# The head of an encoder-layer kernel: inputs and small vectors asked for by GpSimd, own landing tiles for the first projections' weights, and the next weights asked for inside the head

## The chip, the cores and the metric

The kernel runs on one core of one Trainium2 chip. The time is the device time of one execution in microseconds (us), and smaller is better. The kernel before took 2841.35 us (median of three runs, 2839.85 to 2841.55).

## The reference, cut to what matters

One layer of a hybrid encoder is computed for 512 prompt rows and 64 sample rows, each 2048 wide, in float32:

```python
def trunk(x, c, states, params, block):
    ...
        mod = jax.nn.silu(c) @ w_ada[l] + b_ada[l]
        sh1, sc1, g1, sh2, sc2, g2 = jnp.split(mod[:, None, :], N_MOD, axis=-1)
        h = rmsnorm(x, norm1[l]) * (1 + sc1) + sh1
        mix, s_a, s_b, s_c = token_mixers(
            h, gla_s[l], gdn_s[l], conv_s[l], w_in[l], gla_wg[l], gla_bg[l], gla_norm[l],
            gdn_conv_w[l], gdn_a_log[l], gdn_dt_bias[l], gdn_norm[l], w_out[l], block)
        x = x + g1 * mix
        h = rmsnorm(x, norm2[l]) * (1 + sc2) + sh2
        f, s_f = conv_ffn(h, ffn_s[l], w_up[l], ffn_conv_w[l], ffn_conv_b[l], w_down[l])
        x = x + g2 * f
    ...
def token_mixers(h, ...):
    proj = h @ w_in
    (a_q, a_k, a_v, a_r, a_lr, b_q, b_k, b_v, b_g, b_beta, b_alpha) = jnp.split(
        proj, IN_OFFSETS, axis=-1)
    ...
    g = -jnp.exp(gdn_a_log.astype(f32))[:, None, None] * jax.nn.softplus(
        to_heads(b_alpha, GDN_HEADS) + gdn_dt_bias.astype(f32)[:, None, None])
```

Before the first projection `h @ w_in` can start, two of the six parts of `mod` are needed, the shift `sh1` and the scale `sc1`. Each is a product of the two vectors `c` (prompt and sample) with a 2048 x 2048 piece of `w_ada`, so 32 MB of weights are read for two vectors. The other four parts are needed later and are computed beside the projections.

## The kernel before, in words

Activations lie with features on the 128 partitions, so `h` is 16 tiles of 128 x 576 (two halves of 288). Every float32 product is made of three matmuls on pairs of a rounded high part and its rest: `hh` times `wh`, `hl` times `wh`, `hh` times `wl` (function `mm6`, lines 560 and 562, six matmuls of 288 columns for one tile of 128 x 128 weights). A weight tile is loaded to a landing tile, ScalarE makes the high part and VectorE the rest (function `split`, lines 647, 649 and 650).

The first stage is the function `head`. Its work runs in four groups of four feature tiles. For each group g the function `modulation(g)` reads 16 pieces of `w_ada`, 512 KB each (line 751), eight for the scale and eight for the shift; for each piece TensorE makes four matmul instructions with the vectors `c` (line 755). After eight pieces VectorE copies the sum out (line 757), TensorE turns it (line 760), and VectorE adds the bias (line 806). Then `split_mod` forms `hh` and `hl` of the four tiles (lines 582 to 585), and TensorE multiplies them with the narrow columns (`mm_narrow`, line 886) and with the q and k columns of the first head (lines 560 and 562). The x rows are loaded in five blocks (line 697), turned to feature-major by TensorE (line 705), and normed on the way.

The pieces of `w_ada` land in a ring of buffers that is named by the letters of `RING`: `a` is the head's own `hraw` (five buffers), `h` and `l` are the places of split weights `wh` and `wl` (three each), and `r` is the common landing tile `raw` (three). The narrow, q and k weights of a group also land in `raw`.

Before the change all loads and stores of the head are asked for by one queue, SyncE's (SP), in program order as a scheduler lays it out. That scheduler orders each engine's instructions by what it thinks is ready, and `split` raises its own priority by `AHEAD`. An engine then works strictly in that order. A load waits in the queue until its buffer is free, and at most eight transfers of a queue's kind are under way, since each takes one of eight semaphores and waits for the one before it on the same semaphore.

After the head, `gdn_heads` runs the projections head by head, each a `gemm` over 16 tiles. Between the first two, `narrow` makes the decay of all heads: it adds `gdn_dt_bias` to a narrow product, takes a softplus, and sums along the rows by a matmul with a triangle (line 933). `x` is also written to memory for the residual (`xs`, line 799), and `gdn_dt_bias` and `gdn_a_log` are loaded at lines 902 and 903.

## Time and profile before

| what | value |
|---|---|
| median of three runs | 2841.35 us |
| profiled execution | 2845.19 us |
| its span, first to last instruction | 2843.4 us |
| mean granted TensorE clock | 0.988 |
| TensorE busy | 2786.9 us (98%) |
| VectorE busy | 2248.6 us (79%) |
| ScalarE busy | 1293.8 us (46%) |
| GpSimd busy | 316.3 us (11%) |
| moved by DMA | 399.78 MB, mean 141 GB/s |

The page gives the busy time of each engine over the span, then the same in 40 slices. The first two slices (142 us) differ from the rest: there the DMA engines move 322 and 343 GB/s, more than twice what they move later. The later slices have TensorE busy at nine tenths or more. Line numbers are those of the kernel before unless it is said otherwise.

### The profile page before, as it was taken

The page shows a single profiled execution, that of the slowest core. Times are in us where ns is not written, and L with a number is a line of the kernel's source. Part 1 is how long each engine was busy: PE and PEld are TensorE (multiplying, and loading weights), DVE is VectorE, ACT ScalarE, POOL GpSimd, SP SyncE. Part 2 cuts the span into 40 slices and gives each one's busy share as a digit, 9 for nine tenths or more (in the row PEclk, how much of TensorE's full clock was granted, in tenths as well). Part 3 has the DMA queues.
Part 4 walks back from the last instruction along what each step waited for, and adds up shares of the span by engine and source line. Part 5 has one row for each costly group of instructions (what it writes and reads, how often), then busy time and mean ns, then how long its engine had stood idle before and what let it go on. Part 6 is the DMA issues. An engine that isn't in the chain of part 4 may idle for free.

```text
span 2843.4 us, 51759 instructions
## 1 busy us (share of the span) xinstructions
PE 2786.9 (98%) x20560; PEld 2690.0 (95%) x20560; DVE 2248.6 (79%) x3728; ACT 1293.8 (46%) x2285; POOL 316.3 (11%) x586
## 2 busy tenths in 40 slices
PE   7999999999999999999999999999999999999998
PEld 3699999999999999999999999999999999999997
DVE  2488888787777787468888888888878889999995
ACT  4275555444433333255444444444444464434453
POOL 0024433332010001001000000000000000000000
PEclk8999999999999999999999999999999999999999
DMA  9964555555455449333333333333333343443461
GB/s 322 343 189 144 168 155 167 144 154 162 124 149 175 141 143 262 107 111 97 107 105 111 102 104 107 108 104 102 102 104 108 105 151 116 123 124 119 128 171 68
DMA packets 522440, 399.78 MB, mean 141 GB/s; under 512 B 50794, under 2 KB 453957, under 8 KB 522197
## 3 DMA queue, kind: packets, MB, share of 16 engines
q1 hardware_dynamic: 516772, 385.79, 45.7%
q0 software_dynamic: 5424, 10.68, 1.2%
q8 instruction: 162, 2.65, 0.4%
q14 instruction: 82, 0.66, 0.1%
HBM read 356.24 MB, written 40.13 MB: 139 GB/s over the span
## 4 chain that ended last, share of the span: by engine, by line
PE 76%; DVE 4%; DMA 2%; issue 1%; ACT 1%; POOL 0%; SPq 0%; ACTq 0%; DVEq 0%; POOLq 0%
PE g L560 16%; PE g L1381 9%; PE g L1382 8%; PE g L1383 8%; PE g L562 8%; PE bank L1382 3%; PE bank L1381 3%; PE bank L1383 3%; PE g L1616 3%; PE g L1614 3%; PE g L1615 3%; DVE wl L1566 1%; PE bank L1616 1%; PE bank L1614 1%; PE bank L1615 1%
## 5 line engine op out<-in xcount | busy, mean ns | idle before, releaser
L1381 PE MATMUL g<-slot,wh 128*128 128x290 f32 x1760 | 533.4, 303 | 3.1 <-ACT p L1393 3.1
L1382 PE MATMUL g<-slot,wh 128*128 128x290 f32 x1760 | 525.9, 299 | 0.0
L1383 PE MATMUL g<-slot,wl 128*128 128x290 f32 x1760 | 520.4, 296 | 0.0
L560 PE MATMUL g<-hh,wh 128*128 128x288 f32 x1984 | 450.5, 307 | 1.1 <-ACT hh L1168 0.8
L562 PE MATMUL g<-hh,wl 128*128 128x288 f32 x1984 | 432.8, 299 | 0.0
L560 PE MATMUL g<-hl,wh 128*128 128x288 f32 x1984 | 432.1, 298 | 0.0
L1328 ACT ACTIVATE wh<-raw 128x1024 fp32r<-128x1024 f32 x176 | 186.7, 1061 | 391.8 <-PE g L1382 369.5
L1381 PEld LDWEIGHTS g<-slot,wh 128*128 128x128 f32 x1760 | 331.5, 188 | 17.5 <-ACT p L1393 12.0
L1383 PEld LDWEIGHTS g<-slot,wl 128*128 128x128 f32 x1760 | 336.6, 191 | 0.0
L1382 PEld LDWEIGHTS g<-slot,wh 128*128 128x128 f32 x1760 | 335.1, 190 | 0.1
L560 PEld LDWEIGHTS g<-hh,wh 128*128 128x128 f32 x1984 | 320.5, 191 | 3.8 <-ACT hh L1168 1.0
L560 PEld LDWEIGHTS g<-hl,wh 128*128 128x128 f32 x1984 | 322.7, 190 | 0.2 <-issue 0.2
L562 PEld LDWEIGHTS g<-hh,wl 128*128 128x128 f32 x1984 | 321.3, 190 | 0.5 <-DVE wl L650 0.3
L649 ACT ACTIVATE wh<-raw 128x1024 fp32r<-128x1024 f32 x147 | 156.0, 1061 | 313.3 <-PE g L560 284.2
L829 DVE SCALAR_TENSOR_TENSOR acc<-xr,ct,acc 128x512 f32<-128x512 f32 x322 | 230.3, 747 | 1.5 <-DMA xr<-in_w_ada_dram 1.5
L1329 DVE TENSOR_TENSOR wl<-raw,wh 128x1024 fp32r<-128x1024 f32 x176 | 214.5, 1219 | 19.3 <-ACT wh L1328 19.2
L1614 PE MATMUL g<-slot,wh 128*128 128x288 f32 x760 | 224.4, 295 | 0.9 <-DVE slot L1631 0.9
L1616 PE MATMUL g<-slot,wl 128*128 128x288 f32 x760 | 224.0, 295 | 0.3 <-DVE wl L1566 0.3
L1615 PE MATMUL g<-slot,wh 128*128 128x288 f32 x760 | 224.2, 295 | 0.0
L650 DVE TENSOR_TENSOR wl<-raw,wh 128x1024 fp32r<-128x1024 f32 x147 | 179.4, 1221 | 41.8 <-ACT wh L649 41.2
L1382 PE MATMUL bank<-slot,wh 128*128 128x290 f32 x704 | 210.1, 298 | 0.0
L1381 PE MATMUL bank<-slot,wh 128*128 128x290 f32 x704 | 209.4, 297 | 0.0
(418 smaller groups left out, 5926.2 us busy)
## 6 DMA issues: line engine op xcount, KB each, us to landing
raw<-in_w_up_dram SPq DMA_DIRECT2D x176, 512.0 KB
raw<-in_w_in_dram SPq DMA_DIRECT2D x108, 512.0 KB
xr<-in_w_ada_dram SPq DMA_DIRECT2D x86, 512.0 KB
raw<-in_w_down_dram SPq DMA_DIRECT2D x76, 512.0 KB
ax<-in_w_ada_dram SPq DMA_DIRECT2D x42, 512.0 KB
raw<-in_w_out_dram SPq DMA_DIRECT2D x32, 512.0 KB
hraw<-in_w_ada_dram SPq DMA_DIRECT2D x23, 512.0 KB
actd<-v SPq DMA_DIRECT2D x44, 256.0 KB
```

The lines of the kernel that those rows point to most:

```text
L560: T.matmul(ps[:, h if bank is None else bank, :n], wh, x[:, h, :n], start=f, stop=False)
L562: T.matmul(ps[:, h if bank is None else bank, :n], wl, ah[:, h, :n], start=False, stop=stop)
L650: nc.vector.tensor_tensor(lo[:, :n_], raw[:, :n_], hi[:, :n_].bitcast(F32), op=ALU.subtract)
L829: V.scalar_tensor_tensor(acc[s], w[:, k], col, acc[s], op0=ALU.mult, op1=ALU.add)
L1328: self.nc.scalar.activation(hi, src, AF.Copy)
L1329: self.nc.vector.tensor_tensor(lo, src, hi.bitcast(F32), op=ALU.subtract)
L1381: T.matmul(ps, wh[:, j], hi, start=(c < 3 and j == 0), stop=False, skip_group_check=True)
L1382: T.matmul(ps, wh[:, j], lo, start=False, stop=False, skip_group_check=True)
L1383: T.matmul(ps, wl[:, j], hi, start=False, stop=(j == NPAIR - 1), skip_group_check=True)
L1614: T.matmul(ps, wh[:, j, f], hi, start=(c < 3 and j == 0), stop=False, skip_group_check=True)
L1615: T.matmul(ps, wh[:, j, f], lo, start=False, stop=False, skip_group_check=True)
L1616: T.matmul(ps, wl[:, j, f], hi, start=False, stop=(j == n - 1), skip_group_check=True)
```

## The change

- The five blocks of x are asked for by GpSimd's queue, all in the first five steps of the first modulation, instead of by SyncE's in steps 1, 3, 5, 7 and 9. The vectors are asked for by GpSimd too, but for the first group (the two vectors `c`), which ScalarE's queue asks for.
- `RING` is now a finite list of 64 letters: 48 that repeat a pattern of thirteen (four `a`, three each of `h`, `l` and `r`), then 16 without `r`. `hraw` has four buffers instead of five.
- The q and k weights of a group land in a tile kind of their own, `fr`, with four buffers. They are asked for, with the narrow ones, before the pieces of `w_ada` of the next group.
- The split weights of the second head's q projection, both halves, and the first half of its k projection are asked for in group 3 of the head. Before, only the two q halves were, behind the head.
- All writes of `xs` come behind the last piece of `w_ada`. Before, one came in the first group, and the others behind the head.
- `gdn_dt_bias` and `gdn_a_log` are loaded by GpSimd in the head to a tile that lasts (`row8`).
- The copy `rw` of a modulation sum goes to the tile `junk`, which the norms of x also use as a place for values that nobody reads.

```diff
-RING = "ahlarahlahralr"
+RING = "ahlrahlrahlra" * 4
+RING = RING[:48] + "hlahlahlahlahlaa"
...
-                nc.sync.dma_start(rt[at:at + n], ap)
+                (nc.scalar if g == 0 else nc.gpsimd).dma_start(rt[at:at + n], ap)
...
+        self.row8 = self.cp.tile([P, 16], F32, name="row8")
...
-        turns = iter(RING * 99)
+        turns = iter(RING)
...
-            return pool.tile([P, 1024], F32, tag="hraw", bufs=5, name=self.name("hraw"))
+            return pool.tile([P, 1024], F32, tag="hraw", bufs=4, name=self.name("hraw"))
...
+        fraw = lambda: pool.tile([P, 512], F32, tag="fr", bufs=4, name=self.name("fr"))
+        free = [fraw()]
...
-                nc.sync.dma_start(xt[b][q][:n], i["x_prompt"][0, b * P:(b + 1) * P, f] if b < 4 else i["x_sample"][0, :, f])
+                nc.gpsimd.dma_start(xt[b][q][:n], i["x_prompt"][0, b * P:(b + 1) * P, f] if b < 4 else i["x_sample"][0, :, f])
...
-                rw = pool.tile([P, 512], F32, tag="rw", bufs=1, name=self.name("rw"))
+                rw = junk
                 V.tensor_copy(rw, ps)
...
-                for _ in vectors:
-                    pass
             self.scale_mod(s1, 1, "norm1", 4 * g)
...
-            for f, at in ((x_load, 0), (x_turn, X_LAG), (x_norm, X_LAG + 1)):
-                plan[X_AT[b] + at].append(lambda f=f, b=b: f(b))
+            for f, at in ((x_load, b), (x_turn, X_AT[b] + X_LAG), (x_norm, X_AT[b] + X_LAG + 1)):
+                plan[at].append(lambda f=f, b=b: f(b))
         step = iter(plan)
         modulation(0, lambda: [f() for f in next(step)])
+        for c, name in ((0, "gdn_dt_bias"), (8, "gdn_a_log")):
+            nc.gpsimd.dma_start(self.row8[:, c:c + 8], i[name].partition_broadcast(P).rearrange("p a b -> p (a b)"))
+        for _ in vectors:
+            pass
         rx = x_rows()
...
+        self.pre = []
         for g in range(4):
+            ks = range(4 * g, 4 * g + 4)
+            nar = self.narrow_w(pool, 4 * g)
+            ws = [self.split(pool, self.w_in(off)(4 * g, 4 * g + 4), "f", 512, 3, free.pop() if free else fraw())
+                  for off in (OFF_BQ, OFF_BK)]
             if g < 3:
                 modulation(g + 1)
-            ks = range(4 * g, 4 * g + 4)
-            nar = self.narrow_w(pool, 4 * g)
-            qw, kw = [self.split(pool, self.w_in(off)(4 * g, 4 * g + 4), "f", 512, 3) for off in (OFF_BQ, OFF_BK)]
+            else:
+                self.load_consts(None, NARROW)
+                for off, k0 in ((OFF_BQ + P, 0), (OFF_BQ + P, 8), (OFF_BK + P, 0)):
+                    self.pre.append(self.wtile(self.w_in(off)(k0, k0 + 8)))
             for k in ks:
...
-                if k == 0:
-                    nc.sync.dma_start(self.xs[KD - 1], xT[:, KD - 1])
...
-        self.load_consts(None, NARROW)
-        rest = [*range(2, KD - 1), 0, 1]
-        self.pre = []
-        for k0 in (None, 0, 8):
-            if k0 is not None:
-                self.pre.append(self.wtile(self.w_in(OFF_BQ + P)(k0, k0 + 8)))
-                last[0] = self.load_of
-            with self.tc.issue_after(last[0]):
-                for k in rest[:5]:
-                    nc.sync.dma_start(self.xs[k], xT[:, k])
-            rest = rest[5:]
+        with self.tc.issue_after(last[0]):
+            for k in (*range(KD - 3, KD), *range(KD - 3)):
+                nc.sync.dma_start(self.xs[k], xT[:, k])
...
-        row = g("row8", 16)
-        nc.sync.dma_start(row[:, 0:8], i["gdn_dt_bias"].partition_broadcast(P).rearrange("p a b -> p (a b)"))
-        nc.sync.dma_start(row[:, 8:16], i["gdn_a_log"].partition_broadcast(P).rearrange("p a b -> p (a b)"))
+        row = self.row8
```

The scheduler makes new orders of this. Three places matter below. In the rows a name's last number counts allocations, so the same weights bear other numbers in the two kernels.

The first place is SyncE's queue at the start of the program (`hs` are tiles of x; `hraw`, `wh`, `wl` and `raw` hold pieces of `w_ada`). Before:

```order
L751 DMA hraw_214<-in_w_ada_dram 128x2x512
L697 DMA hs_222<-in_x_prompt_dram 128x512
L697 DMA hs_223<-in_x_prompt_dram 128x512
L697 DMA hs_224<-in_x_prompt_dram 128x512
L697 DMA hs_225<-in_x_prompt_dram 128x512
L751 DMA wh_230<-in_w_ada_dram 128x2x512
L751 DMA wl_236<-in_w_ada_dram 128x2x512
```

And now, from the eighth piece of `w_ada` to behind the first weights of the projections:

```order
L755 DMA raw_352<-in_w_ada_dram 128x2x512
L755 DMA hraw_390<-in_w_ada_dram 128x2x512
L755 DMA wh_400<-in_w_ada_dram 128x2x512
L755 DMA wl_430<-in_w_ada_dram 128x2x512
L755 DMA raw_440<-in_w_ada_dram 128x2x512
L648 DMA fr_216<-in_w_in_dram 128x4x128
L648 DMA fr_557<-in_w_in_dram 128x4x128
L755 DMA hraw_468<-in_w_ada_dram 128x2x512
```

Twelve pieces of `w_ada` now stand in a row where x stood between them, and the q and k weights of group 0 come 13th and 14th; x stands in GpSimd's queue behind three vectors and a memset.

The second place is TensorE's order at the third modulation, of group 2 (`bank` is a modulation sum, `fh` and `nar` are weights of the projections). Before, the pieces stand in a row, and the products of group 1 come behind most of them:

```order
L760 MATMUL bank_781<-consts_95,rw_779 128x2 x4
L755 MATMUL bank_787<-wl_788,cst 32x512 x2
L755 MATMUL bank_787<-raw_790,cst 32x512 x2
L755 MATMUL bank_787<-hraw_796,cst 32x512 x2
L755 MATMUL bank_787<-wh_798,cst 32x512 x2
L755 MATMUL bank_787<-wl_804,cst 32x512 x2
L755 MATMUL bank_787<-hraw_806,cst 32x512 x2
L755 MATMUL bank_787<-raw_812,cst 32x512 x2
L560 MATMUL g_542<-hh_848,fh_837 128x288 x2
```

Now the products of group 1 start right behind the turn of its own shift, and the first eight pieces of the next modulation stand singly among them:

```order
L764 MATMUL bank_637<-consts_95,hs_218 128x2 x4
L561 MATMUL g_544<-hh_844,fh_752 128x288 x2
L561 MATMUL ps_k_221<-hh_844,fh_758 128x288 x2
L888 MATMUL g_543<-hh_844,nar_745 66x288 x2
L888 MATMUL g_543<-hl_845,nar_745 66x288 x2
L561 MATMUL g_544<-hl_845,fh_752 128x288
L759 MATMUL bank_763<-wl_764,cst 32x512 x2
L561 MATMUL g_544<-hl_845,fh_752 128x288
L563 MATMUL g_544<-hh_844,fl_753 128x288 x2
L561 MATMUL ps_k_221<-hl_845,fh_758 128x288 x2
L759 MATMUL bank_763<-raw_766,cst 32x512 x2
```

The eight pieces of the shift then stand in a row behind the last product of the group. The order in groups 0 and 2 has the same form.

The third place is TensorE's order behind the head, in the second head's q projection, where the matmul with the triangle (`ln` with `xr`) stands. Before:

```order
L560 MATMUL g_1432<-hh_1125,wh_1288 128x288 x2
L560 MATMUL g_1432<-hl_1126,wh_1288 128x288 x2
L933 MATMUL bank_1384<-ln,xr_1269 128x32
L934 MATMUL bank_1384<-ln,xr_1269 128x4
L562 MATMUL g_1432<-hh_1125,wl_1289 128x288 x2
```

Now:

```order
L563 MATMUL g_1430<-hh_1119,wl_1173 128x288 x2
L561 MATMUL g_1430<-hh_1183,wh_1172 128x288 x2
L933 MATMUL bank_1382<-ln,xr_1163 128x32
L934 MATMUL bank_1382<-ln,xr_1163 128x4
L561 MATMUL g_1430<-hl_1184,wh_1172 128x288 x2
```

It moved back by two rows, to behind the twelfth tile's products and one pair. From the 1675th matmul instruction on (of 19595), TensorE's order is the same in both kernels.

More of the change, by code (lines that the diff above doesn't have):

```diff
@@ L784, in head @@
                 self.h.append((hh, hl))
-                if k == 0:
-                    nc.sync.dma_start(self.xs[KD - 1], xT[:, KD - 1])
                 self.mm_narrow(k, nar[:, k % 4])
-                for ps, w in ((self.ps_q0, qw), (ps_k0, kw)):
+                for ps, w in zip((self.ps_q0, ps_k0), ws):
                     self.mm6(ps, w[0][:, k % 4], w[1][:, k % 4], self.h[k], k == 0, k == KD - 1)
-        self.load_consts(None, NARROW)
-        rest = [*range(2, KD - 1), 0, 1]
-        self.pre = []
-        for k0 in (None, 0, 8):
-            if k0 is not None:
-                self.pre.append(self.wtile(self.w_in(OFF_BQ + P)(k0, k0 + 8)))
-                last[0] = self.load_of
-            with self.tc.issue_after(last[0]):
-                for k in rest[:5]:
-                    nc.sync.dma_start(self.xs[k], xT[:, k])
-            rest = rest[5:]
+        with self.tc.issue_after(last[0]):
+            for k in (*range(KD - 3, KD), *range(KD - 3)):
+                nc.sync.dma_start(self.xs[k], xT[:, k])
         raw = self.xr()
```

## The prediction

> **What bounds the kernel now.** I read the slices of the page first, then stages of the start, then TensorE's (PE) rows in order of time, then the queue's waits. The slices show where PE is not full:
>
> ```profile
> PE   7999999999999999999999999999999999999998
> DMA  9964555555455449333333333333333343443461
> ```
>
> Only the first slices have PE below nine tenths and the DMA engines near full. So I cut the start into stages. A boundary is where the turn of a shift ends (line 760, groups 0 to 3), then the head's last product, then the first transposes of the second head. Columns: PE, weight load, VectorE (DVE), ScalarE (ACT), GpSimd (POOL), granted clock, DMA share, GB/s.
>
> ```profile
> 0.00:10.00 10.00, 3.12 (x9) 1.12 (x10) 0.74 (x6) 2.33 (x5) 1.25 (x7) 1.00 0.60 185
> 10.00:25.00 15.00, 12.80 (x71) 6.11 (x69) 1.38 (x8) 13.11 (x34) 1.11 (x2) 1.00 1.05 395
> 25.00:35.00 10.00, 8.20 (x41) 3.81 (x37) 2.90 (x13) 5.56 (x15) 1.10 (x2) 0.83 0.78 228
> 35.00:48.65 13.65, 12.02 (x62) 4.79 (x64) 3.04 (x8) 3.84 (x12) 0.54 (x1) 0.75 1.03 387
> 48.65:76.97 28.32, 23.88 (x105) 8.97 (x104) 10.33 (x23) 5.31 (x11) 0.00 (x0) 0.76 0.98 351
> 76.97:99.14 22.17, 20.00 (x141) 11.96 (x141) 10.57 (x24) 5.33 (x11) 0.32 (x1) 1.00 1.07 381
> 99.14:125.15 26.01, 24.23 (x162) 14.82 (x163) 10.57 (x24) 5.33 (x11) 0.78 (x2) 1.00 0.98 321
> 125.15:138.36 13.21, 12.72 (x93) 12.01 (x92) 9.59 (x19) 7.96 (x17) 0.00 (x0) 1.00 0.77 274
> 138.36:164.26 25.90, 18.65 (x122) 18.41 (x122) 14.85 (x47) 17.80 (x31) 0.00 (x0) 0.80 0.79 231
> 164.26:300.00 135.74, 135.59 (x1051) 132.15 (x1050) 119.86 (x243) 80.56 (x202) 62.24 (x91) 1.00 0.58 168
> ```
>
> From 164 us on PE does not stop (135.59 of 135.74 us). What the start loses is therefore paid in full, and what it saves arrives at the end, if nothing new waits. Two losses stand out: the loads to 138 us, and the 7.25 us without PE between 138.36 and 164.26. PE's rows for the second (start, length, in brackets the idle time ahead of the row):
>
> ```profile
> 75.92 1.05 PE L760 MATMUL bank<-consts,rw 128*128 128x2 f32 x8 [0.80 <-DVE rw L757]
> 124.20 0.95 PE L760 MATMUL bank<-consts,rw 128*128 128x2 f32 x8
> 137.93 0.43 PE L562 MATMUL ps_k<-hh,fl 128*128 128x288 f32 x2
> 141.19 0.85 PE L560 MATMUL g<-hh,wh 128*128 128x288 f32 x2
> 151.64 0.43 PE L560 MATMUL g<-hl,wh 128*128 128x288 f32 x2
> 157.79 0.61 PE L933 MATMUL bank<-ln,xr 128*128 128x32 f32 x2 [5.72 <-issue]
> 158.64 0.83 PE L562 MATMUL g<-hh,wl 128*128 128x288 f32 x2
> 161.18 0.38 PE L940 MATMUL bank<-cum,xr 128*128 128x36 f32 x2
> ```
>
> The 5.72 us is the triangle matmul. What was late, and what held the queue (SPq) in the head:
>
> ```profile
> 149.80 0.18 DVE L911 COPY dt<-row 128x32 f32<-128x32 f32 x1 [1.38 <-DMA row<-in_gdn_dt_bias_dram]
> 143.37 1.31 SPq L902 DMA_DIRECT2D row<-in_gdn_dt_bias_dram  x1
> 21.83 0.33 SPq L618 DMA_DIRECT2D hs<-in_gdn_conv_w_dram  x1
> 29.36 0.40 SPq L751 DMA_DIRECT2D hraw<-in_w_ada_dram  x1
> 52.33 9.82 SPq L647 DMA_DIRECT2D raw<-in_w_in_dram  x2
> 62.20 0.50 SPq L751 DMA_DIRECT2D hraw<-in_w_ada_dram  x1
> ```
>
> The bias row is asked for at 143.37, behind the stores of x, and lands at 149.80. From 21.83 to 29.36 the queue is taken by nine small vectors, and 25 to 35 us moves 228 GB/s instead of 395. From 52.33 to 62.20 it waits with q and k weights for the shared landing tile.
>
> **The change, part by part.** Prices from rows:
>
> ```profile
> 82.93 0.62 PE L755 MATMUL bank<-raw,cst 128*32 128x512 f32 x2
> 87.41 1.05 PE L760 MATMUL bank<-consts,rw 128*128 128x2 f32 x8 [0.84 <-DVE rw L757]
> 99.75 0.42 PE L886 MATMUL g<-hh,nar 128*66 128x288 f32 x2
> 104.76 0.42 PE L562 MATMUL ps_k<-hh,fl 128*128 128x288 f32 x2
> 117.57 1.05 PE L755 MATMUL bank<-hraw,cst 128*32 128x512 f32 x4
> 118.56 0.54 PE L560 MATMUL g<-hh,fh 128*128 128x288 f32 x2
> 31.37 2.00 PE L622 MATMUL bank<-consts,hs 103*128 103x103 f32 x5
> 125.39 0.72 ACT L583 ACTIVATE hh<-tmp,mod 128x512 fp32r<-128x512 f32 x1 [4.43 <-DVE mod L806]
> 126.54 0.33 ACT L583 ACTIVATE hh<-tmp,mod 128x64 fp32r<-128x64 f32 x1
> 130.92 1.22 DVE L650 TENSOR_TENSOR wl<-raw,wh 128x1024 fp32r<-128x1024 f32 x1
> 151.19 1.28 ACT L924 ACT_TABLE_LOAD   x1
> 186.82 0.77 POOL L357 DMA_DIRECT2D d<-m  x1 [82.39 <-DVE m L1937]
> hraw<-in_w_ada_dram SPq DMA_DIRECT2D x23, 512.0 KB
> hs<-in_x_prompt_dram SPq DMA_DIRECT2D x16, 256.0 KB
> ```
>
> A batch of eight landed pieces takes 82.93 to 86.57 (87.41 less its 0.84 idle): **3.64 us**. A piece that stands alone among other products takes 117.57 to 118.56: **0.99 us**, over twice its share of a batch. Copy and turn: 0.84 + 1.05 = **1.89 us**. The 40 matmuls from 99.75 to 105.18 give **0.136 us** each, and a group has 64 (16 for each of 4 tiles): **8.7 us**. From the turn's end, 125.15, until a whole `hh` is made, 126.87: **1.7 us**.
>
> *Group 0, to the end of its shift.* x and vectors leave SP's queue, so no small transfer stands before a piece, and the 228 GB/s stretch should go. Needed by then: 16 pieces of 512 KB (8.39 MB), x (16 of 256 KB and 4 of half that, 4.72), the first q and k weights (0.52), constants and vectors (some 0.45): 14.1 MB. I leave the first 10 us at 185 GB/s (1.85 MB) and take 395 for the rest: 31.0 us, so landing at 41.0. With one single piece, copy and turn (0.99 + 1.89) it ends at **43.9** instead of 48.65. Low bound 41, if the earlier first pieces fill the first 10 us; high 48.65, if the pace of loads does not change.
>
> *Group 1.* PE now does, in its order: vector transposes (2.0) with the last part of the norm, which now waits for the turn because `rw` and the norm share `junk` (I estimate 1.2 from two short PE, ACT and DVE steps); two single pieces (2.0); 64 products (8.7) with seven more singles (6.9); a turn (1.05); seven pieces in a row (3.2); copy and turn (1.9): **26.9 us**, before 28.3. The 9.82 us queue stall is gone with the own landing tiles, but PE itself is nearly as long.
>
> *Groups 2 and 3.* Products 8.7, eight singles 7.9, copy and turn 1.9, batch 3.6, copy and turn 1.9, wait for `hh` 1.7: **25.7 us** each, before 22.17 and 26.01. Loads need less: 16 pieces and the weights are 9.0 MB, 22.7 us at 395. So PE takes the loads' place as the bound, and this is why I do not expect what the faster loads alone would allow.
>
> Ends of the shifts: 43.9, 70.8, 96.5, 122.2, against 125.15. *The tail* (13.21 us) is a chain through DVE; one more `wl` (1.22) comes in, and about as much DVE idle time can go: unchanged, bounds 12.5 and 14.5. The head ends at 135.4 instead of 138.36: **-3.0**.
>
> *The triangle.* The row is in place long before. PE reaches it after twelve tiles and a pair: before, from 137.93 + 0.43 to 141.19 is 2.83, then to 152.07 is 10.9, plus 0.27: 14.0 us behind the head. The value needs the narrow product, two convolution steps now ahead of it, and three table loads of 1.28 on ACT; by the DVE and ACT orders and their durations I get 15. Stall 1.0 instead of 5.72: **-4.7**, bounds -5.7 (the chain from the bias's copy on took 157.79 - 149.80 = 8.0; started five us behind the head, with the narrow product, it is done before PE comes) and -2 (the three table loads in a row behind the last convolution step). Behind the stall five pairs took 158.64 to 161.18, 2.54 us for 1.36 at full clock: **-1.2**, bounds 0 and -1.2.
>
> What moves to other queues: GpSimd's power steps of the norms now stand behind twenty issues of x (15 us by the 0.77 us row), and the later vectors behind the fourth norm; both are needed only where group 0 ends, at 40 us or later. ScalarE asks for two vectors ahead of its first table load and has nothing else to do then. The ring lets a piece land when the one 13 places ahead of it is used, 6.8 MB or 17 us of loads, so PE's waits of one or two us do not stop it.
>
> The third preloaded tile, earlier stores of `xs` (16 of 288 KB, now beside PE's own work in group 3, where loads wait for PE) and the finite ring cost nothing on this path; without that cover the stores are 4.7 MB, 12 us of DMA, as they were from 128 us on.
>
> **Sum**: -3.0 - 4.7 - 1.2 = -8.9 us. Profiled execution 2845.19 (span 2843.4 and 1.8 around it) becomes 2836.3; it lies 3.8 above the median, so the median goes from 2841.35 to **2832.4**.
>
> **The rivals.** *Loads set the pace (A).* If pieces and products overlap better than my singles, all 64 pieces (33.55 MB) with x, weights and vectors, 40.5 MB, land at 10 + 38.6/0.395 = 107.8, the last shift ends at 110.7, the head at 123.9: -14.5 - 5.9 = -20.4, **2821**. For it: 22.17 us in one group before. Against it: the new PE order, with some 24 singles.
>
> *The moved loads give nothing (B).* If group 0's pace stays, every shift is 4.75 later: -4.1, **2837**. For it: PE is busy 12.02 of 13.65 us to 48.65, at clock 0.75. The Trainium skill, DMA: Bandwidth & Descriptors, Issuing engines are not separate DMA queues, says that transfers asked for by several engines share the same 16 DMA engines and that only issue time is saved; by that rule the sum is this one. Against it: the share was 0.78 between 25 and 35 us, so there was something to fill.
>
> *The triangle still waits (D).* If the longer DVE order keeps 4 to 5 us there: -3.0 - 1.0 = -4.0, **2837**.
>
> *x comes late from GpSimd (C), the slower side.* Twenty loads go through POOL one after the other from about 3 us; the one row of this shape takes 0.77 us, so 15 us in all. PE needs about 9.5 us from the last tile to the turn. Nothing is won from 2.0 us a load on (3 + 40 + 9.5 = 52.5, 8.6 later than my 43.9). At 2.5 us the group ends at 62.5, 18.6 late: **2851**. Against it: 0.77 us, and DVE is busy only 2.1 of the first 25 us. The Trainium skill, SBUF — State Buffer, SBUF: two separate sides, says that VectorE copies in a fast mode lock GpSimd out while it writes the descriptors of its loads; no run here shows that.
>
> **How the numbers follow.** Forecast 0.60, A 0.13, B 0.12, D 0.09, C 0.06. Own range of the forecast: 2827 to 2837. With most of A, all of B and D: 2821 to 2840. A measurement here tells 0.2%, 5.7 us, from no change, so faster means under 2835.7: 0.85 of the forecast, A, and a quarter of B and D: 0.69. Slower than 2847: 0.05. The same: 0.26.
>
> **What would show it.** Right: turns of the shifts near 44, 71, 96 and 122, single pieces of 1 us between products with no DMA wait before them, the triangle's idle time near 1. A is shown by shifts 22 us apart; B by a first shift at 48; C by PE waiting for x tiles; D by 4 us before line 933. A new stall behind 165 us would make the whole sum wrong.

## The result and the profile after

The changed kernel takes 2868.09 us (median of four runs, 2864.72 to 2871.34), the kernel before 2841.28 us beside it (four runs, 2839.85 to 2841.55). The ratio is 1.0095, 95% interval 1.0078 to 1.0113: the change makes the kernel some 27 us slower. I had forecast 2832.4 us, 9 us faster. The profiled execution of the changed kernel took 2866.43 us (span 2864.6), 21.2 us of span more than that of before; that profile lies 3.9 us above its kernel's median, and the changed kernel's 1.7 below.

Stages of the changed kernel, cut as those of before were: the first 35 us, then where the turn of each shift ends (now line 764), then the head's last product, then the second head's first transposes. Columns as before: PE, weight load, DVE, ACT, POOL, granted clock, DMA share, GB/s.

```profile
0.00:10.00 10.00, 0.73 (x2) 0.36 (x2) 0.81 (x6) 1.60 (x3) 6.70 (x16) 1.00 0.82 259
10.00:25.00 15.00, 13.55 (x68) 6.19 (x68) 0.33 (x3) 10.30 (x26) 7.00 (x13) 1.00 1.03 389
25.00:35.00 10.00, 6.34 (x34) 3.65 (x32) 1.33 (x5) 3.30 (x7) 0.55 (x1) 0.83 1.05 293
35.00:51.80 16.80, 12.42 (x65) 4.53 (x63) 4.25 (x14) 10.81 (x32) 8.02 (x16) 0.80 1.06 348
51.80:82.19 30.39, 26.95 (x152) 14.33 (x150) 12.05 (x31) 5.41 (x11) 0.32 (x1) 0.89 0.97 326
82.19:110.75 28.56, 25.18 (x144) 13.33 (x144) 10.36 (x24) 5.09 (x11) 0.32 (x1) 0.94 0.83 272
110.75:140.36 29.61, 26.23 (x145) 14.23 (x144) 10.36 (x24) 5.10 (x11) 0.00 (x0) 0.88 0.87 267
140.36:153.41 13.05, 10.59 (x65) 10.08 (x64) 10.31 (x19) 8.09 (x16) 0.52 (x1) 0.87 1.03 379
153.41:171.97 18.56, 16.17 (x114) 15.93 (x115) 12.10 (x43) 14.45 (x29) 0.00 (x0) 0.91 0.72 190
171.97:300.00 128.03, 118.28 (x868) 114.89 (x867) 98.65 (x205) 68.47 (x178) 42.34 (x78) 0.95 0.52 148
```

Three parts make up the 21.2 us:

| stage | before | forecast | after | after less before |
|---|---|---|---|---|
| group 0, to the end of its shift | 48.65 | 43.9 | 51.80 | +3.15 |
| groups 1, 2, 3 | 28.32, 22.17, 26.01 | 26.9, 25.7, 25.7 | 30.39, 28.56, 29.61 | +12.06 |
| tail of the head | 13.21 | 13.2 | 13.05 | -0.16 |
| head end to the second head's transposes | 25.90 | 20.0 | 18.56 | -7.34 |
| from there to the end of the span | 2679.1 | as before | 2692.6 | +13.5 |

The last row is a loss where I expected nothing. Before, TensorE was busy 135.59 of 135.74 us there; now it lacks 9.75 of 128.03 us up to 300. TensorE, POOL, DVE and ACT rows of the changed kernel in order of time:

```profile
199.21 0.57 POOL L358 DMA_DIRECT2D d<-m  x1 [47.08 <-DVE m L1937]
...
216.65 0.16 DVE L1937 TENSOR_TENSOR rk<-nbe,s 128x4 f32<-128x4 f32 x1
230.65 0.69 DVE L386 TENSOR_TENSOR m<-cm,consts 128x512 f32<-128x512 f32 x1 [13.84 <-DMA cm<-d]
231.45 1.28 ACT L1937 ACTIVATE m<-m,s 128x128 f32<-128x128 f32 x4 [17.95 <-DVE s L1937]
234.31 0.70 PE L561 MATMUL g<-hh,wh 128*128 128x288 f32 x2 [3.47 <-ACT wh L650]
238.52 0.85 PE L563 MATMUL g<-hh,wl 128*128 128x288 f32 x2 [3.02 <-DVE wl L651]
257.69 1.36 PE L253 MATMUL bank<-m,m 128*128 128x64 f32 x8 [3.01 <-DVE m L1937]
```

`cm` is the result of the 16 x 16 inverses, which GpSimd starts at 199.21 and whose last transfer lands at 230.65. VectorE comes to the mask that reads it at 216.8 and stands for 13.84 us, ScalarE behind VectorE for 17.95, and TensorE runs out of split weights: 3.47 + 3.02, and 3.01 at the next step of the same chain. VectorE's order explains it. Before, the first mask was the 286th instruction of VectorE in the trace, behind some twenty rows of `acc` and `wl` work that other engines want (the last rows ahead of it):

```
L829 SCALAR_TENSOR_TENSOR acc_2143<-xr_2334,ct,acc_2143 128x512
L650 TENSOR_TENSOR wl_2488<-raw_2486,wh_2487 128x1024
L997 COPY gcb<-g_2152 128x64
L385 TENSOR_TENSOR m_2406<-cm_2280,consts_1311 128x512
```

And now it is the 260th, 26 places earlier, ahead of all of that work:

```
L1937 TENSOR_TENSOR s_291_1897<-s_291_1897 128x4
L1937 TENSOR_TENSOR rk_2029<-nbe,s_291_1897 128x4
L386 TENSOR_TENSOR m_2398<-cm_2272,consts_1312 128x512
```

Nothing in the diff touches this place.

In the head, the rows that carry the loss (timeline of the changed kernel, groups 0, 1 and 3):

```profile
13.53 0.54 POOL L701 DMA_DIRECT2D hs<-in_x_prompt_dram  x1 [0.45 <-DMA hs<-in_x_prompt_dram]
14.58 0.54 POOL L701 DMA_DIRECT2D hs<-in_x_prompt_dram  x1 [0.51 <-DMA hs<-in_x_prompt_dram]
...
13.91 3.23 SPq L755 DMA_DIRECT2D wl<-in_w_ada_dram  x1
17.19 3.50 SPq L755 DMA_DIRECT2D raw<-in_w_ada_dram  x1
20.73 8.71 SPq L648 DMA_DIRECT2D fr<-in_w_in_dram  x2
...
29.63 1.89 PE L759 MATMUL bank<-raw,cst 128*32 128x512 f32 x4 [3.66 <-DMA raw<-in_w_ada_dram]
32.17 0.60 ACT L712 ACTIVATE xT<-g 128x512 f32<-128x512 f32 x1 [5.79 <-PE g L709]
39.23 0.55 POOL L145 TENSOR_TENSOR rs<-rs,mhalf 128x1 f32<-128x1 f32 x1 [13.27 <-DVE rs L144]
44.30 2.04 PE L736 MATMUL g<-hs,consts 128*128 128x512 f32 x2 [3.50 <-DVE hs L731]
53.50 0.30 PE L623 MATMUL bank<-consts,hs 88*128 88x88 f32 x1 [0.96 <-DMA hs<-in_ffn_conv_b_dram]
55.30 0.35 PE L623 MATMUL bank<-consts,hs 72*128 72x72 f32 x1 [1.50 <-DMA hs<-in_state_gdn_conv_dram]
...
112.53 0.85 PE L561 MATMUL g<-hh,fh 128*128 128x288 f32 x2 [1.77 <-ACT hh L584]
114.99 1.92 PE L759 MATMUL bank<-wh,cst 128*32 128x512 f32 x4
120.80 0.43 PE L563 MATMUL g<-hh,fl 128*128 128x288 f32 x2
121.16 1.05 PE L759 MATMUL bank<-hraw,cst 128*32 128x512 f32 x4
122.14 0.53 PE L561 MATMUL ps_k<-hh,fh 128*128 128x288 f32 x2
122.51 0.43 PE L561 MATMUL ps_k<-hl,fh 128*128 128x288 f32 x2
...
168.57 0.38 PE L933 MATMUL bank<-ln,xr 128*128 128x32 f32 x2 [0.86 <-issue]
```

*Group 0.* TensorE starts late: it waits 4.03 us, until 8.46, for a vector that GpSimd asked for (before, 0.68 us, until 4.85). While x streams through GpSimd, one load of 256 KB in about 1.05 us, SyncE gets a piece of 512 KB off only every 3.2 to 3.7 us. Then the q and k weights of group 0 hold SyncE's queue for 8.71 us. TensorE stands 3.66 us for a piece; the transposes of x stand behind that piece in its order, ScalarE waits 5.79 us for them, the norms stand behind on ScalarE, GpSimd waits 13.27 us for the third norm, and TensorE waits 3.50 us at line 736 for the result. Three pieces, a copy and the turn still stand behind that, at a granted clock of 0.61 (44.3 to 51.8 us). *Group 1* adds 0.96 and 1.50 us of waits for vectors, which stand behind the norms in GpSimd's queue. *Group 3* in three stretches (the wait and the low clock, the rest of the products, the batch):

```profile
110.75:119.73 8.98, 7.21 (x25) 4.10 (x25) 6.83 (x16) 4.47 (x10) 0.00 (x0) 0.62 0.80 287
119.73:133.08 13.35, 13.35 (x74) 7.26 (x72) 0.00 (x0) 0.00 (x0) 0.00 (x0) 1.00 0.76 246
133.08:140.36 7.28, 5.67 (x48) 2.87 (x48) 3.52 (x8) 0.63 (x1) 0.00 (x0) 1.00 1.15 283
```

In the middle stretch TensorE is full and the loads are at 246 GB/s: TensorE sets the pace, as forecast, but more slowly. From 120.80 to 122.51 two pairs of products (0.264 us each at this clock) and one single piece pass in 1.71 us, so a single costs 1.18 us, not 0.99. And behind the 1.77 us wait the granted clock is 0.62.

### The profile page after: what moved, and what is told of

It is laid out like the page before. It is cut to its first block, busy times and chain, and to the rows that moved or that the text cites. A ratio compares the mean times of both kernels' runs of the same rounds, so it can differ in the third digit from the quotient of the medians.

```text
span 2864.6 us, 51780 instructions
## 1 busy us (share of the span) xinstructions
PE 2793.7 (98%) x20560; PEld 2695.2 (94%) x20560; DVE 2248.8 (79%) x3728; ACT 1292.1 (45%) x2284; POOL 336.2 (12%) x620
## 4 chain that ended last, share of the span: by engine, by line
PE 75%; DVE 5%; DMA 2%; issue 1%; ACT 1%; POOL 0%; SPq 0%; ACTq 0%; DVEq 0%; POOLq 0%
PE g L561 16%; PE g L1381 9%; PE g L1382 8%; PE g L1383 8%; PE g L563 8%; PE bank L1382 3%; PE bank L1381 3%; PE bank L1383 3%; PE g L1614 2%; PE g L1616 2%; PE g L1615 2%; DVE wl L1566 1%; PE bank L1615 1%; PE bank L1614 1%; PE bank L1616 1%
## 5 line engine op out<-in xcount | busy, mean ns | idle before, releaser
L650 ACT ACTIVATE wh<-raw 128x1024 fp32r<-128x1024 f32 x147 | 155.7, 1060 | 286.0 <-PE g L561 257.4
```

## The experiments

The kernel before was timed beside the experiments: its median is 2843.47 us beside e1 to e4, 2841.73 beside e5 to e8, 2841.95 beside e10 to e13, and 2842.83 beside e14 and e15. The table has each profile's stages: end of the first shift, groups 1 to 3 together, end of the head, TensorE's stall ahead of the triangle (line 933), and the time from the second head's first transposes to the end ("rest"). The ratio is to the kernel before beside it, with its 95% interval.

| kernel | 1st shift | groups 1-3 | head end | triangle | rest | median | ratio |
|---|---|---|---|---|---|---|---|
| before | 48.65 | 76.5 | 138.4 | 5.72 | 2679.1 | 2841.28 | |
| the change | 51.80 | 88.6 | 153.4 | 0.86 | 2692.6 | 2868.09 | 1.0095 (1.0078 to 1.0113) |
| e1_row_alone | 49.65 | 77.4 | 140.0 | 4.00 | 2692.5 | 2857.49 | 1.0049 (1.0034 to 1.0064) |
| e2_row_masks | 50.10 | 76.8 | 140.1 | 3.59 | 2678.2 | 2848.88 | 1.0016 (1.0007 to 1.0026) |
| e3_change_masks | 53.77 | 88.4 | 155.6 | 0.76 | 2680.6 | 2858.94 | 1.0061 (1.0038 to 1.0083) |
| e4_change_x_sp | 48.65 | 90.5 | 152.2 | 0.80 | 2686.7 | 2858.29 | 1.0054 (1.0039 to 1.0069) |
| e5_products_first | 54.66 | 84.5 | 150.7 | 2.31 | 2685.3 | 2856.60 | 1.0046 (1.0029 to 1.0062) |
| e6_products_first_x_sp | 49.84 | 84.1 | 146.4 | 2.31 | 2679.4 | 2852.56 | 1.0036 (1.0024 to 1.0048) |
| e7_two_preloads | 46.72 | 91.1 | 150.8 | 0.77 | 2685.6 | 2856.64 | one run |
| e8_row_late | 51.17 | 88.8 | 153.0 | 2.13 | 2691.0 | 2865.61 | one run |
| e10_before_w_early | 53.77 | 84.6 | 150.4 | 4.01 | 2677.6 | 2852.95 | 1.0042 (1.0028 to 1.0057) |
| e11_before_x_gpsimd | 52.13 | 72.5 | 138.1 | 4.33 | 2683.8 | 2847.21 | 1.0015 (1.0005 to 1.0024) |
| e12_change_w_late | 49.83 | 81.3 | 146.8 | 0.75 | 2683.8 | 2852.33 | 1.0038 (1.0023 to 1.0053) |
| e13_w_late_x_sp | 48.10 | 83.4 | 147.2 | 2.31 | 2685.2 | 2854.37 | 1.0046 (1.0031 to 1.0061) |
| e14_row_tile_before_stores | 50.20 | 77.9 | 142.3 | 4.48 | 2683.4 | 2849.24 | 1.0022 (1.0012 to 1.0031) |
| e15_before_products_first | 56.44 | 87.7 | 155.7 | 1.77 | 2683.5 | 2852.76 | 1.0037 (1.0023 to 1.0051) |

None of them beats the kernel before. The stages are those of one profiled execution, which isn't always near the median: e2's is the fastest of its ten runs (2844.15 us), e15's the slowest of its five (2862.91).

### The masks that stand ahead of their data: e1, e2, e3

`e1_row_alone` is the kernel before with one part of the change, the early bias row:

```diff
+        for c, name in ((0, "gdn_dt_bias"), (8, "gdn_a_log")):
+            nc.gpsimd.dma_start(self.row8[:, c:c + 8], i[name].partition_broadcast(P).rearrange("p a b -> p (a b)"))
         rx = x_rows()
...
-        row = g("row8", 16)
-        nc.sync.dma_start(row[:, 0:8], i["gdn_dt_bias"].partition_broadcast(P).rearrange("p a b -> p (a b)"))
-        nc.sync.dma_start(row[:, 8:16], i["gdn_a_log"].partition_broadcast(P).rearrange("p a b -> p (a b)"))
+        row = self.row8
```

> Kernel before, with one part of the change alone: the bias row (gdn_dt_bias, gdn_a_log) is loaded by GpSimd in the head to a lasting tile. Theory M (the early row lets the scheduler order VectorE otherwise: the two masks of the first 16 x 16 inverses stand 26 rows earlier in VectorE's order, ahead of the data they wait for, and VectorE, then ScalarE, then TensorE run dry behind them): the triangle's stall of 5.72 us goes and TensorE reaches the second head's first transposes near 157 instead of 164.3 (-7.3), but VectorE then waits 10 to 15 us for cm and TensorE stands 9 to 10 us, with a lower clock behind it (+13.5 in the changed kernel): about 2841.3 - 7.3 + 13.5 = 2847.5 us. Rival R (the late stall of the changed kernel comes from another part of it: the third preloaded tile, the stores of xs, GpSimd's other work): the row gives its gain alone, 2841.3 - 7.3 = 2834 us, with no stall of VectorE behind 200 us.

`e2_row_masks` (on e1) and `e3_change_masks` (on the whole change) queue the two masks on VectorE behind the last `wl`. The scheduler then moves a few other rows near that place too, on VectorE, ScalarE, TensorE and SyncE:

```diff
-        for w, x in enumerate((t, u)):
-            nc.vector.tensor_tensor(x.rearrange("p b (n j) -> p b n j", n=8), cm[:, w].unsqueeze(2).to_broadcast(sh),
+        with self.tc.issue_after(self.wl_of):
+            for w, x in enumerate((t, u)):
+                nc.vector.tensor_tensor(x.rearrange("p b (n j) -> p b n j", n=8), cm[:, w].unsqueeze(2).to_broadcast(sh),
...
             nc.vector.tensor_tensor(lo[:, :n_], raw[:, :n_], hi[:, :n_].bitcast(F32), op=ALU.subtract)
+            self.wl_of = nc.cur_bb.bb.instructions[-1]
```

> The kernel of the run before it, and the two masks of an inverse are queued on VectorE behind the last rest wl that was asked for ahead of them (an order alone, no wait on data); they stand at row 280 of VectorE's order, where the kernel before has them at 282. Theory M: the stall of VectorE for cm is 3 us or less, TensorE does not run dry, and the gain of the early row is left: 2841.3 - 7.3 = 2834 us, 2832 to 2837. Rival R: the place of the masks does nothing, the time is that of the row alone.

> The whole change, with the two masks queued behind the last rest wl as in the run before (row 277 of VectorE's order instead of 253). Theory M: the three stalls of TensorE between 230 and 258 us (3.47, 3.02 and 3.01) go with the low clock behind them, 13.5 us in all: 2868.1 - 13.5 = 2854.6 us, the rest of the loss (the head's 15.0 less the triangle's 7.3) stays. Rival R: TensorE runs dry all the same because the whole start is later, 2868 us.

Of the row alone, VectorE's mask and TensorE's waits behind 172 us (waiter, releaser: total, times, longest):

```profile
220.51 0.69 DVE L385 TENSOR_TENSOR m<-cm,consts 128x512 f32<-128x512 f32 x1 [11.75 <-DMA cm<-d]
```

```profile
PE bank L252 <- DVE m L1938: 3.9, 1, 3.9
PE g L562 <- DVE wl L650: 3.4, 1, 3.4
PE g L560 <- ACT wh L649: 0.8, 1, 0.8
```

With the masks held back, the same two places:

```profile
228.22 0.69 DVE L386 TENSOR_TENSOR m<-cm,consts 128x512 f32<-128x512 f32 x1 [4.18 <-DMA cm<-d]
239.14 1.71 PE L252 MATMUL bank<-m,m 128*128 128x64 f32 x8 [2.30 <-DVE m L1940]
```

Theory M held for the late stall: the row alone brings it (8.1 us on TensorE), an edit that names nothing but the place of the two masks takes it to 2.3 us in e2, and in the whole change from 9.5 to 3.4. The other rows that moved with the masks weren't held in place: one `wh` of ScalarE, for one, stands two rows earlier, ahead of 0.58 and 0.21 us of work in e2. In the table, the two profiles with the masks early have a rest of 2692.5 and 2692.6 us; the thirteen other experiments have 2677.6 to 2691.0, mean 2683.4. So the masks cost some 9 us: 6 of TensorE's waits, and the rest, as far as this spread allows, the lower clock behind them (0.90 granted from 230 to 300 us in the change, 0.98 in e3, 1.00 before). The medians say the same: 8.6 us from e1 to e2, 9.2 from the change to e3.

What missed: the early row did not bring its 7.3 us (e1 is 10 us above its expected 2847.5, e2 15 above 2834), and e3 is 4 above its 2854.6. The triangle's stall fell only from 5.72 to 4.00 and 3.59; this is taken up below. Even with the masks held back, the early row is 5.4 us slower than the kernel before by the medians, and e2's one profile, faster than that of before, doesn't show where.

### x through GpSimd: e4, e11

`e4_change_x_sp` is e3 with the loads of x and the vectors given back to SyncE, `e11_before_x_gpsimd` the kernel before with the loads of x alone given to GpSimd:

```diff
-                nc.sync.dma_start(xt[b][q][:n], i["x_prompt"][0, b * P:(b + 1) * P, f] if b < 4 else i["x_sample"][0, :, f])
+                nc.gpsimd.dma_start(xt[b][q][:n], i["x_prompt"][0, b * P:(b + 1) * P, f] if b < 4 else i["x_sample"][0, :, f])
...
-            for f, at in ((x_load, 0), (x_turn, X_LAG), (x_norm, X_LAG + 1)):
-                plan[X_AT[b] + at].append(lambda f=f, b=b: f(b))
+            for f, at in ((x_load, b), (x_turn, X_AT[b] + X_LAG), (x_norm, X_AT[b] + X_LAG + 1)):
+                plan[at].append(lambda f=f, b=b: f(b))
```

> The run before (whole change, masks held back), with x and all vectors asked for by SyncE again, in the steps of the kernel before (1, 3, 5, 7, 9); the weights of the projections are still asked for early, with landing tiles of their own. Theory H (two losses in the head: x through GpSimd takes the bandwidth of the pieces and its norms come late, 3.2 us until the first shift; and the early weights break the batches of pieces into single pieces among products with a low clock, 12 us in groups 1 to 3): the first shift's turn ends near 49 instead of 51.8, groups 1, 2 and 3 stay at 28 to 30 us each, 2854.6 - 3 = 2851.6 us. Rival X (the x loads on GpSimd are behind all of the head's loss): the groups fall back to 28, 22 and 26 us and the head ends near 138, 2840 us.

> The kernel before with one edit: x is asked for by GpSimd in the first five steps, as in the change; the vectors stay with SyncE. Theory V (x through GpSimd does not speed up the first shift but makes it uncertain: 46.7, 51.2, 51.8, 53.8 and 54.7 us in five profiles with the GpSimd loads against 48.65 to 50.1 in five without): the first shift ends between 46 and 55, groups 1 to 3 stay near 76.5, the time is 2842 to 2846 us and its spread is larger than that of the kernel before. Rival G (GpSimd's loads are behind the head's loss): 2848 us or more. My forecast on record gave this edit -4.75 us: 2837 us.

e4: the first shift is back at 48.65, groups 1 to 3 stay at 90.5: theory H's stages held, rival X fell. The time is 7 above the expected 2851.6, with a rest of 2686.7. e11: the first shift comes at 52.13, and group 1 behind it is shorter (24.26 against 28.32 us), so the head ends at 138.1 as before. Theory V held in the head. Its time, 2847.2, lies between V's range and rival G's 2848, and its spread (2842.30 to 2849.23) is no larger than that of the kernel before beside it (2838.41 to 2845.85). By its one profile the loss lies in the rest, not in the head; why is open. The 4.75 us that my forecast gave this edit are not there. Leaving out e10 and e15, whose first weights wait for the shared landing tile ahead of pieces in SyncE's queue, the first shift ends at 46.7 to 54.7 with x from GpSimd (seven, mean 51.4) and at 48.1 to 50.2 without (seven, mean 49.3).

### Asking early for the weights: e10, e12, e13

`e10_before_w_early` is the kernel before with five lines in another order:

```diff
-            if g < 3:
-                modulation(g + 1)
             ks = range(4 * g, 4 * g + 4)
             nar = self.narrow_w(pool, 4 * g)
             qw, kw = [self.split(pool, self.w_in(off)(4 * g, 4 * g + 4), "f", 512, 3) for off in (OFF_BQ, OFF_BK)]
+            if g < 3:
+                modulation(g + 1)
```

`e12_change_w_late` does the reverse to e3 (the modulation ahead of the weights again); `e13_w_late_x_sp` does it to e4.

> The kernel before with one edit: the narrow, q and k weights of a group are asked for ahead of the next modulation in the program instead of behind it (same ring, same landing tile raw, x and vectors on SyncE). The scheduler then sets six to eight single pieces among the products of groups 1 to 3, much as in the changed kernel. Theory W (asking early makes the singles, and these and the low clock make the groups long): groups 1, 2 and 3 take 84 to 90 us together instead of 76.5, the time is 2841.7 + 7 to 13 = 2851 us. Rival G (the head's loss comes from GpSimd's loads, the ring or the landing tiles): 76 to 78 us, 2842 us.

> The whole change with the masks held back, and the narrow, q and k weights asked for behind the next modulation, as in the kernel before; they keep their own landing tiles. The scheduler's order then has batches again in parts (five, eight, three and seven pieces in a row) and about half of the singles. Theory W: groups 1 to 3 take 78 to 84 us instead of 88 to 91, ScalarE's norms of x no longer stand behind a weight that has not landed, 2858.9 - 8 = 2851 us. Rival G: 88 us or more, 2858 us.

> The run before it with x and the vectors on SyncE again: what is left of the change is the ring, the landing tiles, the three preloaded tiles, the early bias row and the late stores of x, with the masks held back. Theory W: first shift near 49, groups 1 to 3 78 to 82 us, head end near 141 to 143, triangle 0.8 to 2.3 us, 3 us at the masks: 2843 to 2848 us. Rival G (the loss sits in the ring or the landing tiles): groups of 88 us, 2855 us or more.

The three groups of e10, from shift to shift:

```profile
53.77:81.10 27.33, 25.20 (x145) 13.22 (x144) 9.18 (x22) 3.74 (x8) 0.32 (x1) 0.92 0.79 280
81.10:109.65 28.55, 25.10 (x144) 14.02 (x144) 10.35 (x24) 5.61 (x12) 0.78 (x2) 0.88 0.88 314
109.65:138.37 28.72, 25.30 (x145) 13.24 (x144) 10.36 (x24) 5.09 (x11) 0.00 (x0) 0.94 0.89 318
```

Theory W held for the groups on both sides: this one edit takes the kernel before from 76.5 to 84.6 us in groups 1 to 3, with about the TensorE time, the clock and the DMA rate of the changed kernel, and 11 us in all; undone in the change it brings 88.4 down to 81.3 (e12), 2858.94 to 2852.33 us in time. In e10 the first shift is also later (53.77), since the weights of group 0 now stand ahead of pieces in SyncE's queue, where the second of them waits for a landing tile from 36.38 to 42.72. e13 missed: its groups are a little above their 78 to 82 us, and its 2854.37 us are 6 above theory W's range and next to rival G's 2855. What stays open is why e12 and e13 remain at 81 and 83 us: their order still has half the singles, but ring and landing tiles were not taken apart.

### Products first: e5, e6, e15

`e5_products_first` is e3 with the next modulation written behind the products of a group, so that pieces come in batches of eight; e6 the same on e4, `e15_before_products_first` on the kernel before with early weights.

```diff
-            if g < 3:
-                modulation(g + 1)
-            else:
+            if g == 3:
                 self.load_consts(None, NARROW)
...
                 for ps, w in zip((self.ps_q0, ps_k0), ws):
                     self.mm6(ps, w[0][:, k % 4], w[1][:, k % 4], self.h[k], k == 0, k == KD - 1)
+            if g < 3:
+                modulation(g + 1)
```

> The whole change with the masks held back (e3_change_masks), and the modulation of the next group stands behind the products of a group in the program instead of ahead of them. Queues, loads, landing tiles and ring stay; TensorE now does the 64 products of a group in a row and then the pieces in batches of eight. Theory S (the groups are 28 to 30 us long because single pieces stand among the products): a group is 8.7 (products) + 2 x (3.64 + 1.89) (batches and turns) + 1.8 (wait for hh) = 21.5 us of TensorE's time, and its 9.0 MB of loads take 22.8 us at 395 GB/s; some waits on loads come in, so 23 to 25 us; the head ends 13 to 18 us earlier, near 140, and the time is 2858.9 - 15 = 2844 us. Rival L (the loads set the pace in the changed kernel too, at the 250 to 300 GB/s of its groups 2 and 3): TensorE waits on loads for what it saves, groups stay at 28 to 30 us, 2857 us or more.

> The run before, with x and the vectors asked for by SyncE as in the kernel before (as e4_change_x_sp had it). Theory S: the first shift's turn ends near 49 (48.65 in the kernel before and in e4_change_x_sp) instead of 52 to 54, groups 1 to 3 take 23 to 25 us each, the head ends near 135, the triangle waits 0.8 us and about 3 us are lost at the masks: 2843 - 3 (head) - 5 (triangle) + 3 = 2838 us. Rival L: groups of 28 to 30 us, 2855 us.

> The kernel before with the weights of a group asked for early (as e10_before_w_early) and the next modulation behind the products in the program, so that the pieces stay in batches of eight. Theory W1 (the singles alone make early asking cost): groups 1 to 3 take 70 to 76 us, 2836 to 2842 us. Theory W2 (with the products in a row no piece is used meanwhile, so the ring's 14 places fill, the loads stop and then come one by one; with them stand the weights and preloads ahead of the pieces): groups 1 to 3 take 80 to 86 us as in e5 and e6 (84.5 and 84.1), 2846 to 2852 us.

SyncE's queue in e15, in group 1:

```profile
58.19 0.71 SPq L751 DMA_DIRECT2D raw<-in_w_ada_dram  x1
70.94 4.95 SPq L647 DMA_DIRECT2D raw<-in_w_in_dram  x2
75.94 0.50 SPq L751 DMA_DIRECT2D hraw<-in_w_ada_dram  x1
```

From 58.90 to 70.94 nothing is asked for: twelve pieces lie unused in the ring, next in the queue stand q and k weights that wait for a landing tile `raw` with one of these pieces in it, and TensorE does products. From 71 to 76 us the loads are down to 54 GB/s, and TensorE then waits 9.1 us for single pieces over the three groups. That is theory W2, though 87.7 and 2852.76 us lie a little above its ranges. In e5 the same happens in group 1 alone (30 and 0 GB/s between 65 and 75 us). In e6 the loads hardly stop:

```profile
49.84:79.54 29.70, 24.39 (x152) 15.66 (x151) 13.09 (x33) 6.34 (x14) 0.32 (x1) 0.88 1.03 346
79.54:104.54 25.00, 21.41 (x145) 14.64 (x144) 10.48 (x24) 5.21 (x11) 0.32 (x1) 0.87 1.07 360
104.54:133.91 29.37, 24.45 (x145) 13.99 (x144) 13.98 (x27) 8.38 (x14) 0.00 (x0) 0.94 1.07 371
```

There the DMA engines are full, and they carry more in these stages, 30.2 MB by these rates against 26.7 in the kernel before. So theory S and W1 fell. Rival L came near in time (e5 2856.60, e6 2852.56), but not at the 250 to 300 GB/s that it named, and in e6 TensorE waits only 4.0 us for pieces and is busy 70.3 of 84.1 us at a clock of 0.87 to 0.94. How e6's groups divide between transfers and TensorE's own work stays open. Only group 2 of e5 and e6 came down to 25 us. In these runs early weights cost either way; that late weights let TensorE use up pieces while the weights are on their way is how I read it, and no run shows it alone.

### The triangle: e7, e8, e14

`e7_two_preloads` and `e8_row_late` are e3 with, in turn, the third tile of the second head and the early row undone (in e8 the two loads of the row stand again at the place that e1 removed); e14 is e2 with the third tile asked for ahead of the stores of x.

```diff
-                for off, k0 in ((OFF_BQ + P, 0), (OFF_BQ + P, 8), (OFF_BK + P, 0)):
+                for off, k0 in ((OFF_BQ + P, 0), (OFF_BQ + P, 8)):
```

> The whole change with the masks held back, and two tiles of the second head are asked for in group 3 as in the kernel before, not three: the first half of its k projection is split behind the head again. Theory A (the triangle's wait has two parents: the bias row, and ScalarE, which in its order stands before the split of a tile that has not landed; the row alone moved the stall from 5.72 to 4.00): TensorE waits 3 to 5 us for line 933's input again, and ScalarE waits 3 us or more for raw ahead of it. Rival (the row alone is behind it, and the 4.00 us of the row-alone run come from that run's shorter head): the stall stays at 0.8 us.

> The whole change with the masks held back and three tiles asked for early, but the bias row is loaded by SyncE behind the stores of x, as in the kernel before. Theory A (two parents): VectorE waits for the row again and the triangle's stall is back at 3 to 6 us. Rival (the third tile alone took the stall away): it stays at 0.8 us.

The edit of e14:

```diff
-        for k0 in (None, 0, 8):
-            if k0 is not None:
-                self.pre.append(self.wtile(self.w_in(OFF_BQ + P)(k0, k0 + 8)))
-                last[0] = self.load_of
-            with self.tc.issue_after(last[0]):
-                for k in rest[:5]:
-                    nc.sync.dma_start(self.xs[k], xT[:, k])
-            rest = rest[5:]
+        for off, k0 in ((OFF_BQ + P, 0), (OFF_BQ + P, 8), (OFF_BK + P, 0)):
+            self.pre.append(self.wtile(self.w_in(off)(k0, k0 + 8)))
+        with self.tc.issue_after(self.load_of):
+            for k in rest:
+                nc.sync.dma_start(self.xs[k], xT[:, k])
```

> The kernel before with the early bias row, the masks held back (both as in e2_row_masks), and a third tile of the second head (the first half of its k projection) asked for ahead of the stores of x, which all come behind it. Theory A2 (the triangle's second parent is ScalarE's wait for that tile: it is asked for behind the stores, and in the changed kernel it came in time only because the longer head let the stores finish, also with two preloads): the value for line 933 is ready 15 us behind the head instead of 17.9, the stall is 1 us or less, and 2 to 3.5 us are left at the masks: 2842 - 5.7 + 3 = 2839 us, 2836 to 2842. Rival (the length of the chain behind the narrow product sets it, whatever ScalarE waits for): the stall stays at 3.5 to 4 us, 2845 to 2849 us as e2_row_masks.

What stands ahead of the triangle's value, in the row-alone run:

```profile
147.91 1.06 ACT L649 ACTIVATE wh<-raw 128x1024 fp32r<-128x1024 f32 x1 [3.72 <-DMA raw<-in_w_in_dram]
```

and in e14:

```profile
158.88 0.49 DVE L829 TENSOR_SCALAR acc<-xr,ct 128x512 f32<-128x512 f32 x1 [2.06 <-DMA xr<-in_w_ada_dram]
```

Behind the head's end the triangle's matmul comes after 19.4 us in the kernel before, 18.3 in e1, 17.3 in e14, 16.4 in e8, and 15.1 to 15.2 in the change, e3 and e7. Theory A fell: with two preloads the stall stays at 0.77, and in e8 it is 2.13, below A's 3 to 6. So did theory A2 in its narrow form: with the tile ahead of the stores, ScalarE no longer waits, but the value is still 17.3 us behind, since VectorE now waits for the next load behind the stores. The stall of 4.48 also has a second part: TensorE comes to line 933 12.8 us behind the head in e14, and 14.3 in e1 and in the change.

What agrees with all the runs is wider: some load that stands behind the stores of x is late, and stands in some engine's order ahead of the triangle's chain. The traces sort the sixteen kernels by when SyncE asks for the last store of x. In the nine where that is 1.8 us or more ahead of the head's end, the matmul comes 15.1 to 15.6 us behind the head; in e8, where it is 1.4 ahead, 16.4; in the six where it is at the head's end or up to 1.7 us behind it, 17.3 to 19.4. The length of the head isn't it: the head of e10 ends at 150.4, as late as that of e7, but e10's stores are asked for only from 10.2 us ahead of that end (e7's from 15.7), and its stall is 4.01. Nor is the early row needed for most of it: e15 asks for the row behind the stores like the kernel before, at 156.15, 0.5 us behind the head's end, but its last store 5.4 us ahead of that end, and the stall is 1.77. This last step is argued from the traces; no run changed the stores alone. In e8 the row has its part, since VectorE waits 1.93 us for it.

## Why the prediction was wrong, point by point

- **What bounds the start.** Right as far as the traces show: TensorE, not the loads, sets the pace of groups 2 and 3 in the changed order (272 and 267 GB/s there). That the start is paid in full fits the stages, within the spread of the rest.
- **Group 0: 43.9 forecast, 51.80 measured.** The step that failed is "I leave the first 10 us at 185 GB/s (1.85 MB) and take 395 for the rest: 31.0 us, so landing at 41.0". The bytes were nearly in time: by the rates (259 GB/s for 10 us, 389 for 15, 293 for 10, 362 from 35 to 41) 13.5 MB had moved by 41.0, against the 14.1 that I counted. But they came in another order, x first and the pieces at half their rate, and the sum had only loads behind one another. TensorE, ScalarE and GpSimd each stood in order behind what was late, and three pieces still stood behind the norm's result at 44.30. Rival B (the moved loads give nothing) is what e11 shows: the head ends where it did. The rule of the Trainium skill, DMA: Bandwidth & Descriptors, Issuing engines are not separate DMA queues, agrees with that run: the head ends at 138.1 against 138.4 us. Rival C's condition, 2 us a load, did not come: a load of x takes 0.54 us to issue, and the last is asked for at 23.1. Its sign came once, at the start: TensorE waits 2.29 us for x until 11.20. The lock-out of GpSimd that the Trainium skill, SBUF — State Buffer, SBUF: two separate sides, names is shown by no row: the gaps between these issues end with a landed load, of x or of a vector.
- **Group 1: 26.9 forecast, 30.39 measured.** I had the vectors "needed only where group 0 ends". They stood behind the fourth norm, which was late itself: 2.66 us of waits (0.96, 1.50 and one of 0.20), and a clock of 0.89 that I had not counted.
- **Groups 2 and 3: 25.7 forecast, 28.56 and 29.61 measured.** The mechanism was right (singles among the products), two sizes were off. "A piece that stands alone among other products takes 117.57 to 118.56" (0.99 us) leaves out the gaps on both sides; 1.18 us each make 1.5 us in a group. And the products were priced at the full clock: in group 3, to 119.73, TensorE did 16 products (2.1 us) and two singles (2.4) in 7.2 us, 2.7 more, at 0.62. I had these groups 1.6 us longer than before on average; they are 5.0 longer.
- **The tail, 13.2 forecast:** 13.05. Right.
- **The triangle, 1.0 forecast and -4.7:** 0.86 and -4.86. Both terms came (TensorE 14.3 us behind the head for 14.0, the value 15.2 for 15), but the reason is half of it. By e1 the row alone takes 1.7 us off. I had left out the weights of ScalarE and VectorE that wait behind the stores of x; in the changed kernel they were in time because the last store is asked for 2.6 us ahead of the head's end. That it came out was in part luck.
- **The sum.** "What it saves arrives at the end, if nothing new waits" held as a condition, and a new stall behind 165 us was named as what would make the sum wrong. I had read the new orders of VectorE and ScalarE only as far as line 933. The row that moved up by 26 places stands behind it, and it turned the early row, the part of the change of whose gain I was surest, into a loss of 9 us by the spread of the table (13.5 in the profiled pair). None of the rivals had it.

## What to carry to other kernels

When a scheduler lays out the order, an input that comes earlier moves other instructions too: compare the position of each instruction that waits for another engine over the whole program, above all those of an engine that feeds TensorE, not only around the edit. Asking earlier for weights is not free where the engine that uses them also empties the ring of another stream: price the interleaved order with its gaps and its clock, or the ring while it is full. And a stall that shrinks is not yet the gain of the edit that was aimed at it: ask which other parts moved the loads ahead of it.

## What the runs showed of the hardware

- With GpSimd's and SyncE's queues both streaming, x moved 256 KB in about 1.05 us (some 250 GB/s) and the pieces 512 KB in 3.2 to 3.7 us (some 150): the two queues shared about 390 GB/s (389 from 10 to 25 us) unevenly. The first shift's end lay 8 us apart in the profiles of the seven kernels with x from GpSimd (46.7 to 54.7), and 2.1 us in the seven without.
- Behind waits of 0.79, 0.81 and 1.77 us the granted clock was 0.62 over 9 us in group 3, where the kernel before, with no wait over 0.84 us in groups 2 and 3, kept 1.00.
- The rest of the program, some 2680 us, took 2677.6 to 2691.0 us in profiles of kernels without the late stall: a few us of difference between two single profiles say little.
